# Fourteen of the mixer's sixteen transposed column blocks as seven block products, run beside the attention's steps, their results spilled to memory

## The chip, the cores and the metric

The kernel runs on one NeuronCore of a Trainium2 chip. The metric is the device time of one execution in microseconds (us). The kernel before takes 3112.58 us, the median of three runs (3110.77 to 3117.67).

The engines that matter here are PE (TensorE, the matrix products; PEld is its loading of weights), DVE (VectorE), ACT (ScalarE), POOL (GpSimd) and SP (SyncE, which issues most DMAs). Each works through its own instructions in a fixed order, and waits on semaphores for the others.

## The reference

Two layers, each a SwiGLU feed-forward network (FFN), a mixer and a second FFN, with RMS norms and per-sequence modulation around each. 640 tokens go through: 512 of a prompt and 8 x 16 of sampled sequences. D_MODEL is 1024. Of one mixer this matters:

```python
z = h @ w_in[l]                                   # (640, 1024) @ (1024, 5128)
q, k, v = z[AQ], z[AK], z[AV]                     # 512 columns each: attention, 4 heads
o_a = rmsnorm(attention(q, k, v, past_k, past_v)) # prompt: 512 tokens; sampled: 8 sequences on 256 past rows each
qk = silu(causal_conv(z[MQ : MV], conv0))         # 1024 columns: short convolution over tokens
vm, og = z[MV], sigmoid(z[MO])                    # 512 columns each
o_m = rmsnorm(og * mlstm(qk, vm, z[MI], z[MF], c0, n0, m0))   # 4 memory heads, new states returned
g = sigmoid(z[G])                                 # 2048 columns: a gate for each branch
y = (g[:1024] * (o_a @ w_pa[l]) + g[1024:] * (o_m @ w_pb[l])) @ w_out[l]
```

## The kernel before

**Numbers.** All products are in fp32 accuracy: both operands are split into a high part `hi` and a rest `lo`, and `three` (its matmuls appear at L91 or L80) adds hi*hi, hi*lo and lo*hi. The split of a weight tile is a copy on ACT and a subtraction on DVE (L300 for 128x1024, L330 and L495 for 128x512).

**Two ways to compute transposed columns.** Of `z`, the columns AQ, AK, MQ, MK and G are computed transposed (channels on partitions, tokens along the free dimension): 32 blocks of 128 columns, that is sixteen pairs of 256. `columns` computes a block plainly: for each of the two token halves of 320 it adds 8 x 3 matmuls of 128x320, so 48 per block and 96 per pair. The FFN has another way, `blocks` (L733): it cuts a pair's product into 2x2 blocks (tokens, columns, and the 1024 channels in halves of 512) and computes seven block products in place of eight, with sums on DVE and POOL before and after; a pair then takes 7 x 12 = 84 matmuls of 128x320. For this it needs sums of the input's blocks, which `split_half` and `combine` make (tiles `t42` and `t13`; the second fills the eight C tiles).

**One mixer's order.** In the program: AQ and AK of the first two heads, `values(0)` (token-major columns, and the gates MI and MF), the 8 prompt steps of the heads 0 and 1, AQ and AK of the heads 2 and 3, the other 8 prompt steps and the 8 sampled steps; `gate_columns(0)`; `values(1)`; MQ and MK columns, each followed by its convolution (`conv`); `values(2)`; `memory_gates`; the branch `w_pa`, with `gated`; the four memory heads (`memory_head`, `values(3)` within); `gate_columns(1)`; the branch `w_pb`, with `merge`; and `out_projection` with `w_out`. A scheduler orders each engine's instructions by this program and by priorities, so columns that stand later in the program fill PE between dependent steps that stand earlier. Tiles come from rings: `acc` and `bank` (PSUM), S (42 tiles), K (4 tiles of 128x320, `half`), W, X, C and raw; an instruction that takes a tile waits until the last reader of its predecessor in the ring is done.

**A memory head** is a chain of dependent parts: rows of the gates on PE, weights on DVE and ACT, five products `bank<-S,S` (queries by keys), the products with the values `bank<-S,Fv` and `bank<-X,Fp`, a norm on DVE, ACT and POOL, transposes (L1390), two copies to C tiles, and only then its part of `w_pb`. The new states (`bank<-S,Fa`, then L1430 on DVE, then a store) follow.

## Time and profile before

| | us |
|---|---|
| median of three runs | 3112.58 |
| the profiled execution | 3114.34 |
| its span | 3112.6 |
| mixer of layer 0, first column matmul to first `w_out` matmul (551.19 to 1055.34) | 504.1 |

The mean granted TensorE clock is 0.991. The mixer of layer 1 stands at about 2095 to 2600 us of the span and has the same shape. Within the mixer of layer 0, the sampled steps stand alone on PE from about 801 to 825 us, the convolutions run from about 831 us, the memory heads from 909.71 us, and `w_pb` from 1025 us. A stretch in which PE is busy for its whole length is bound by PE; where PE is idle, the releaser in brackets tells what it waited for. The busy time of a stretch counts overlapping rows once; the groups' busy times add them up.

### The profile page before, as it was taken

What the parts mean: (1) busy time and instruction counts of PE and PEld (TensorE: products, weight loads), DVE (VectorE), ACT (ScalarE), POOL (GpSimd) and SP (SyncE); (2) the same over time, 40 slices, a digit from 0 to 9 for tenths busy, and PEclk for the clock granted to TensorE, in tenths of its full rate; (3) what the DMA queues carried; (4) which work ended last, traced back from release to release, by engine and by line L of the source; (5) the groups of instructions that cost most, each with busy time, mean ns of one, the idle gap of its engine ahead of it and who ended that gap; (6) DMA issues with size and microseconds to landing.
All of it is one profiled execution on the core that took longest, in us unless ns stands there. A gap on an engine that the chain in (4) does not pass through costs nothing.

```text
span 3112.6 us, 51071 instructions
## 1 busy us (share of the span) xinstructions
PE 3014.8 (97%) x19101; PEld 2691.6 (86%) x19101; DVE 2002.8 (64%) x3745; ACT 1360.5 (44%) x2829; POOL 1040.5 (33%) x987
## 2 busy tenths in 40 slices
PE   6999999999999989999999999999999999899998
PEld 5888877999899979998778888879998998899986
DVE  5686557444675588785776665673446646887755
ACT  5333346344424364444643333562343334644454
POOL 3474304110111066660355552031001112676502
PEclk9999999999999999999999999999999999999999
DMA  7555536223323443334554555461233244333335
GB/s 231 159 177 167 186 125 219 88 79 92 116 77 115 131 161 109 122 106 139 177 183 155 172 164 170 140 215 55 82 99 106 77 124 156 104 89 89 105 126 176
DMA packets 307961, 417.47 MB, mean 134 GB/s; under 512 B 22235, under 2 KB 208967, under 8 KB 307714
## 3 DMA queue, kind: packets, MB, share of 16 engines
q1 hardware_dynamic: 303026, 402.78, 41.7%
q0 software_dynamic: 4688, 11.43, 1.1%
q8 instruction: 151, 2.47, 0.3%
q14 instruction: 96, 0.79, 0.1%
HBM read 386.98 MB, written 27.14 MB: 133 GB/s over the span
## 4 chain that ended last, share of the span: by engine, by line
PE 88%; DVE 5%; DMA 3%; ACT 2%; issue 1%; POOL 1%; SPq 0%; POOLq 0%; DVEq 0%; ACTq 0%
PE acc L91 53%; PE bank L91 29%; PE acc L80 4%; DMA raw<-in_w_ffn_dram 1%; DVE W L300 1%; ACT W L299 1%; DMA raw<-in_w_in_dram 1%; PE bank L1095 0%; DMA Fv<-in_w_ada_dram 0%; DVE S L495 0%; DMA S<-in_w_ada_dram 0%; PE bank L526 0%; DMA raw<-in_w_out_dram 0%; DVE S L556 0%; DVE X L593 0%
## 5 line engine op out<-in xcount | busy, mean ns | idle before, releaser
L91 PE MATMUL acc<-S,W 128*128 128x320 f32 x4640 | 747.4, 314 | 2.3 <-DVE dm L1182 1.6
L91 PEld LDWEIGHTS acc<-S,W 128*128 128x128 f32 x4640 | 688.7, 188 | 54.8 <-issue 22.7
L300 DVE TENSOR_TENSOR W<-raw,W 128x1024 fp32r<-128x1024 f32 x240 | 307.5, 1283 | 284.4 <-ACT W L299 282.9
L91 PE MATMUL acc<-W,C 128*128 128x512 f32 x1848 | 445.0, 400 | 15.0 <-DVE W L300 11.3
L91 PEld LDWEIGHTS acc<-W,C 128*128 128x128 f32 x1848 | 347.7, 190 | 109.6 <-DVE W L300 18.5
L299 ACT CAST W<-raw 128x1024 fp32r<-128x1024 f32 x248 | 259.7, 1048 | 358.8 <-PE acc L91 267.4
L495 DVE TENSOR_TENSOR W<-raw,W 128x512 fp32r<-128x512 f32 (+1 forms) x244 | 220.4, 904 | 153.2 <-ACT W L494 136.7
L91 PE MATMUL bank<-S,X 128*128 128x320 f32 x1936 | 315.4, 311 | 0.0
L91 PEld LDWEIGHTS bank<-S,X 128*128 128x128 f32 x1936 | 291.3, 188 | 10.9 <-issue 9.2
L91 PE MATMUL acc<-C,W 128*128 128x320 f32 x1728 | 274.1, 311 | 0.0
L91 PEld LDWEIGHTS acc<-C,W 128*128 128x128 f32 x1728 | 258.3, 188 | 5.1 <-issue 5.0
L801 POOL TENSOR_TENSOR S<-S,K 128x320 f32<-128x320 f32 x160 | 173.5, 1100 | 243.6 <-DVE K L800 238.4
L494 ACT CAST W<-raw 128x512 fp32r<-128x512 f32 (+1 forms) x244 | 150.7, 618 | 166.7 <-PE bank L91 77.6
L494 ACT CAST C<-S 128x384 fp32r<-128x384 f32 (+2 forms) x280 | 134.8, 490 | 126.4 <-PE acc L91 86.6
L495 POOL TENSOR_TENSOR C<-S,C 128x256 fp32r<-128x256 f32 x44 | 54.8, 1248 | 392.3 <-ACT C L494 391.8
L91 PE MATMUL bank<-W,C 128*128 128x512 f32 x792 | 185.1, 395 | 0.0
L91 PEld LDWEIGHTS bank<-W,C 128*128 128x128 f32 x792 | 149.0, 188 | 35.5
L495 DVE TENSOR_TENSOR X<-raw,X 128x512 fp32r<-128x512 f32 x160 | 161.5, 1011 | 25.6 <-ACT X L494 25.2
L451 POOL TENSOR_TENSOR sm<-sm,mhalf 128x1 f32<-128x1 f32 (+2 forms) x80 | 60.7, 759 | 345.3 <-DVE sm L446 175.6
L91 PE MATMUL acc<-S,X 128*128 128x320 f32 x976 | 166.4, 312 | 0.0
L91 PEld LDWEIGHTS acc<-S,X 128*128 128x128 f32 x976 | 148.2, 188 | 17.8 <-issue 10.9
L494 ACT CAST X<-raw 128x512 fp32r<-128x512 f32 (+1 forms) x164 | 100.6, 615 | 138.2 <-PE bank L91 92.5
(382 smaller groups left out, 5091.3 us busy)
## 6 DMA issues: line engine op xcount, KB each, us to landing
raw<-in_w_ffn_dram SPq DMA_DIRECT2D x348, 512.0 KB, 4.0
Fv<-in_w_ada_dram SPq DMA_DIRECT2D x261, 256.0 KB, 3.2
raw<-in_w_in_dram SPq DMA_DIRECT2D x72, 512.0 KB, 4.2
raw<-in_w_out_dram SPq DMA_DIRECT2D x32, 512.0 KB, 4.6
x<-X SPq DMA_DIRECT2D x25, 512.0 KB, 3.2
X<-x SPq DMA_DIRECT2D x25, 512.0 KB, 4.3
raw<-in_w_in_dram SPq DMA_DIRECT2D x32, 256.0 KB, 3.8
X<-in_cache_k_dram SPq DMA_DIRECT2D x16, 512.0 KB, 5.7
```

The costliest lines, as they stand in the source:

```text
L80: i = PE.matmul(out, lhsT, rhs, start=start and first is None, stop=stop and last is not None).ins
L91: i = PE.matmul(out, lhsT, rhs, start=start, stop=stop).ins
L299: ACT.copy(hi, src)
L300: (eng or DVE).tensor_tensor(lo, src, hi.bitcast(F32), ALU.subtract)
L451: pows.append(POOL.tensor_tensor(r, t, mhalf.to_broadcast([P, n]), ALU.pow).ins)
L494: ACT.copy(hi, src)
L495: (eng or DVE).tensor_tensor(lo, src, hi.bitcast(F32), ALU.subtract)
L801: POOL.tensor_tensor(gm, gm, z, ALU.mult)
```

## The change

**Which columns.** Only the first pair of AQ and the first of AK stay plain (`first_columns`, with weights that are split early). The other fourteen pairs (AQ and AK of the heads 2 and 3, all of G, MQ and MK) go through `blocks(..., apart=True)`: its weights take W tiles alone, its sums an X tile, its products `acc` tiles alone. `pre_norm` therefore always leaves the plain sum in `x`, and `split_half` and `combine` run for the mixer too, as for the FFN.

**Where they run.** `side_blocks` is a generator with two turns per pair. One turn is taken after each turn of the attention's steps (`turns` is the old `pipeline`, turn by turn): four before `values(0)` of the attention's second half, and the rest beside the remaining prompt steps and all sampled steps.

**Where the results go.** AQ and AK stay in S tiles. The gates' tanh (16 blocks) and the convolution's input (8 blocks) are written to memory in halves of 128x320 (160 KB) by SP (`to_memory`, through a K tile), and loaded back as 320 KB tiles by `gated`, `merge` and `conv`. Since the C tiles hold the block sums until the last pair is done, the attention's normed rows are put aside in memory by POOL's queue (`put_aside`, six per layer), and `attention_out` loads, transposes and splits them after the stage. The tables of masks are loaded in two lots. S tiles become 645 wide.

**What follows later.** History, `values(0)`, both `conv`, `values(1)`, `attention_out`, `memory_gates`, `conv_rows`, `values(2)`, `w_pa`, the memory heads (with `values(3)`) and `w_pb` stand after the stage, without MQ, MK and gate columns among them.

Counted over the program, PE has 336 fewer matmuls of 128x320, DVE 3873 rows in place of 3666, ACT 2537 in place of 2446, POOL 1083 in place of 951, and SP 1157 in place of 993 (among them 96 stores of 160 KB and 48 loads of 320 KB).

```diff
+    def combined(h):
+        for k in range(HK):
+            h["t42", k] = O(), O()
+            h["t4", k], h["t2", k] = ([z[:, c] for z in h["t42", k]] for c in halves_of_tokens)
+            h["t13", k] = C(), C()
+            h["t1", k], h["t3", k] = ([z[:, c] for z in h["t13", k]] for c in halves_of_tokens)
+        return h
...
-    def blocks(src, h, put):
+    def blocks(src, h, put, apart=False):
...
-            x = WX((P, 2 * HK, P), F32R)
+            x = (W if apart else WX)((P, 2 * HK, P), F32R)
             hl = x[:, :HK], x[:, HK:]
             split_to(hl, t, eng)
-            out = product_bank()
+            out = acc()[:, :TA] if apart else product_bank()
...
+        if apart:
+            s12 = X((P, 2 * HK, P))
+            s1, s2 = s12[:, :HK], s12[:, HK:]
+        else:
+            s1, s2 = (F("a").rearrange("p (k c) -> p k c", k=HK) for _ in range(2))
...
+        def first_columns(puts):
+            ws = list(zip(puts, first_weights["mixer", l]))
+            for t in range(2):
+                for put, w in ws:
+                    b = acc()[:, :TA]
+                    proj_t(b, w, h, t)
+                    put(t, b)
...
+        def to_memory(dst, m0, finish=None):
+            def put(m, t, x, y, over):
+                z = x if over else half()
+                DVE.tensor_tensor(z, x, y, ALU.add)
+                if finish:
+                    finish(z)
+                load(dst[m0 + m][:, halves_of_tokens[t]], z)
+            return put
+        gate = [spilled(f"tanh_{br}", KD) for br in range(2)]
+        pre = spilled("pre", KD)
+        def side_blocks():
+            def keep(dst, scale=None):
+                def put(m, t, x, y, over):
+                    if 2 + m not in dst:
+                        dst[2 + m] = L()
+                    o = dst[2 + m][:, halves_of_tokens[t]]
+                    DVE.tensor_tensor(o, x, y, ALU.add)
+                    if scale:
+                        ACT.activation(o, o, AF.Copy, scale=scale[2 + m])
+                return put
+            def half_tanh(z):
+                ACT.activation(z, z, AF.Tanh, scale=0.5)
+            parts = [(OFF_AQ + 256, keep(q, qscale)), (OFF_AK + 256, keep(k))]
+            parts += [(OFF_G + DM * br + P * m, to_memory(gate[br], m, half_tanh)) for br in range(2) for m in range(0, KD, 2)]
+            parts += [(OFF_MQ + P * m, to_memory(pre, m)) for m in range(0, KD, 2)]
+            for off, put in parts:
+                yield from blocks(wl[:, off:off + 256], h, put, apart=True)
...
+        def put_aside(j):
+            aux(aside[j], rms_rows(obs[j]))
...
-            xn = rms_rows(obs[hd])
-            yield
-            tr = rows_t(xn)
-            oa[hd] = C(), C()
-            ACT.activation(oa[hd][0][:, :SEQ], tr, AF.Copy, scale=na)
-            DVE.scalar_tensor_tensor(oa[hd][1][:, :SEQ], tr, na, oa[hd][0][:, :SEQ].bitcast(F32), ALU.mult, ALU.subtract)
+            put_aside(hd)
...
+        def attention_out():
+            for hd in range(NH):
+                xn = F("a")
+                load(xn, aside[hd])
+                tr = rows_t(xn)
...
+            for m in range(4):
                 mm_ = base + m
-                if not half:
-                    zt[m] = L(), mk(per, [P, 152], "dm", 1)
-                z, zs = zt[m]
-                zs = zs.rearrange("p (b t) -> p b t", b=SB)
-                if not half:
-                    POOL.memset(z[:, 0:3], 0.0)
-                    POOL.tensor_copy(zs[:, :, 0:3], hT[:, mm_].rearrange("p (b j) -> p b j", b=SB))
-                    ACT.copy(z[:, 3:3 + TA], b)
-                    return
-                ACT.copy(z[:, 3 + TA:515], b[:, :SEQ - TA])
-                DVE.tensor_copy(zs[:, :, 3:], b16(b[:, SEQ - TA:]))
+                z, zs = L((P, 3 + TOK)), once([P, 152], "dm").rearrange("p (b t) -> p b t", b=SB)
+                POOL.memset(z[:, 0:3], 0.0)
+                load(z[:, 3:], pre[mm_])
+                POOL.tensor_copy(zs[:, :, 0:3], hT[:, mm_].rearrange("p (b j) -> p b j", b=SB))
+                DVE.tensor_copy(zs[:, :, 3:], b16(z[:, 3 + SEQ:]))
...
-        attn_columns(0)
-        values(0)
-        history()
+        attn_columns()
+        attn_values(0)
         for hd in (0, 1):
             head_rows(hd)
-        pipeline([prompt_step(hd, i) for hd in (0, 1) for i in range(4)])
-        attn_columns(1)
+        steps = turns([prompt_step(hd, i) for hd in range(NH) for i in range(4)] + [sampled_step(b) for b in range(SB)])
+        side = side_blocks()
+        for n in range(4):
+            next(side)
+            next(steps)
+        attn_values(1)
         for hd in (2, 3):
             head_rows(hd)
         key_rows(NH)
-        pipeline([prompt_step(hd, i) for hd in (2, 3) for i in range(4)] + [sampled_step(b) for b in range(SB)])
-        ta = gate_columns(0)
+        for _ in itertools.zip_longest(side, steps):
+            pass
+        history()
+        _, _, tri = table(1)
+        tri_b, mask_w, mask_wb, mask_t, mask_tb = table(2)
+        values(0)
+        conv(0, qm, 0.5)
         values(1)
-        columns(*halves_at(OFF_MQ, 512, conv(0, qm, 0.5)))
-        columns(*halves_at(OFF_MK, 512, conv(4, km, 0.5 * KSCALE)))
-        values(2)
+        conv(4, km, 0.5 * KSCALE)
+        attention_out()
         mem = memory_gates()
         conv_rows()
+        values(2)
         def gated(m, a, b):
+            ta[m] = L()
+            load(ta[m], gate[0][m])
...
-        tb = gate_columns(1)
-        h2 = new_rows()
+        h2 = plain_rows()
         def merge(m, a, b):
+            tb = L()
+            load(tb, gate[1][m])
```

**PE beside a prompt step** (layer 0). Before: between a step's transposes and scores (`bank`) stand plain columns of AQ for the heads 2 and 3, `acc_6673`, from the input's tiles `S`, and their weights `W`.

```order
L91 MATMUL acc_6673<-S_4140,W_6668 128x320
L91 MATMUL acc_6673<-S_4142,W_6667 128x320
L1053 MATMUL bank_6327<-ident_63,Fp_6310 128x128 x2
L91 MATMUL bank_6334<-S_5817,S_5763 128x384
L91 MATMUL bank_6338<-S_5817,S_5763 128x384
L91 MATMUL acc_6673<-S_4143,W_6667 128x320
L91 MATMUL acc_6673<-S_4142,W_6668 128x320
L91 MATMUL acc_6673<-S_4144,W_6667 128x320
```

After, the same kind of step (`bank_6949` is its transpose, `bank_6956` and `bank_6960` its scores):

```order
L91 MATMUL acc_7016<-S_4158,W_7013 128x320
L91 MATMUL acc_7016<-S_4160,W_7013 128x320
L91 MATMUL acc_7016<-S_4161,W_7013 128x320
L1073 MATMUL bank_6949<-ident_63,Fp_6869 128x128 x2
L91 MATMUL bank_6956<-S_5835,S_5781 128x384
L91 MATMUL bank_6960<-S_5835,S_5781 128x384
L91 MATMUL acc_7016<-S_4160,W_7013 128x320
L91 MATMUL acc_7035<-S_4162,W_7032 128x320
L91 MATMUL acc_7035<-S_4163,W_7032 128x320
```

The filling matmuls are now those of block products: a product is twelve matmuls, so `acc_7016` ends here, and `acc_7035` begins the next one with another split weight tile.

**VectorE at the end of `values(0)` of the memory.** Before: the splits of the next column block's weights (`W_6546`, `W_6605`) stand around the copies of the five token tiles (`acc_6090` to `bank_6094`), and nothing of the convolution is near.

```order
L330 TENSOR_TENSOR W_6546<-raw_6541,W_6545 128x512
L330 TENSOR_TENSOR W_6546<-raw_6543,W_6545 128x512
L986 COPY S_6231<-acc_6090 128x128
L986 COPY S_6231<-acc_6091 128x128
L986 COPY S_6231<-acc_6092 128x128
L989 TENSOR_TENSOR gt_5728<-acc_6090,bif_5729 128x8
L986 COPY S_6231<-acc_6093 128x128
L989 TENSOR_TENSOR gt_5728<-acc_6091,bif_5729 128x8
L986 COPY S_6231<-bank_6094 128x128
L989 TENSOR_TENSOR gt_5728<-acc_6092,bif_5729 128x8
L1158 COPY S_5736<-bank_6251 128x192
L330 TENSOR_TENSOR W_6605<-raw_6541,W_6604 128x512
```

After, `S_9416` is a convolution input loaded from memory, and `S_9424` its sum:

```order
L299 TENSOR_TENSOR W_9499<-raw_9495,W_9498 128x1024
L1001 COPY S_9396<-acc_9255 128x128
L1001 COPY S_9396<-acc_9256 128x128
L1001 COPY S_9396<-acc_9257 128x128
L1004 TENSOR_TENSOR gt_5714<-acc_9255,bif_5715 128x8
L1001 COPY S_9396<-acc_9258 128x128
L1004 TENSOR_TENSOR gt_5714<-acc_9256,bif_5715 128x8
L1001 COPY S_9396<-bank_9259 128x128
L1004 TENSOR_TENSOR gt_5714<-acc_9257,bif_5715 128x8
L299 TENSOR_TENSOR W_9566<-raw_9562,W_9565 128x1024
L1203 COPY dm_9417<-S_9416 128x8x16
L1210 TENSOR_SCALAR S_9424<-S_9416,cwb_5728 128x512
```

The convolution's first instructions (L1203, L1210) stand behind the copies L1001 of `values(0)`, while their input comes from memory.

**PE in the memory heads.** Before, in the last two heads: `bank` tiles are the heads' own products and transposes, `acc_10529` a gate column block.

```order
L91 MATMUL bank_10101<-S_8681,S_8995 128x128
L91 MATMUL acc_10529<-S_4144,W_10523 128x320
L91 MATMUL acc_10529<-S_4145,W_10523 128x320
L91 MATMUL acc_10529<-S_4144,W_10524 128x320
L91 MATMUL bank_10106<-S_8681,S_8995 128x128
L91 MATMUL acc_10529<-S_4146,W_10523 128x320
L91 MATMUL bank_10111<-S_6232,Fa_10109 128x128 x4
L91 MATMUL bank_10111<-ws_9279,S_6232 128x1 x4
L91 MATMUL bank_10111<-wsm_9283,S_6232 128x8
L1400 MATMUL bank_10129<-ident_63,S_8839 128x128 x4
L1400 MATMUL bank_10135<-ident_63,S_8839 128x128
L1390 MATMUL bank_10140<-ident_63,S_9144 128x128 x4
```

After, head 2: `bank_10765` to `bank_10787` are its five products `S,S`, `bank_10812` its products with the values, and `acc_11260` a part of `w_pb` for head 0.

```order
L91 MATMUL acc_11260<-C_10527,W_11219 128x320
L91 MATMUL acc_11260<-C_10526,W_11220 128x320
L91 MATMUL bank_10765<-S_9462,S_9690 128x512
L91 MATMUL bank_10771<-S_9462,S_9690 128x384
L91 MATMUL bank_10777<-S_9462,S_9690 128x256
L91 MATMUL bank_10782<-S_9462,S_9690 128x128
L91 MATMUL bank_10787<-S_9462,S_9690 128x128
L1420 MATMUL bank_10790<-ident_63,S_9652 128x128 x4
L1420 MATMUL bank_10796<-ident_63,S_9652 128x128
L1410 MATMUL bank_10801<-ident_63,S_9630 128x128 x4
L1410 MATMUL bank_10808<-ident_63,S_9630 128x128
L91 MATMUL bank_10812<-S_10092,Fv_10759 128x129 x2
```

The column blocks between a head's parts are gone; what is left between them is other heads' own work and the first heads' part of `w_pb`.

## Rows read from the trace of the kernel before

**Rows 1.** The page of the profile: busy time by engine, and the chain that ended last
```profile
PE 3014.8 (97%) x19101; PEld 2691.6 (86%) x19101; DVE 2002.8 (64%) x3745; ACT 1360.5 (44%) x2829; POOL 1040.5 (33%) x987
...
PE 88%; DVE 5%; DMA 3%; ACT 2%; issue 1%; POOL 1%; SPq 0%; POOLq 0%; DVEq 0%; ACTq 0%
```

**Rows 2.** Busy time by stretch: start:end, length, PE, PEld, DVE, ACT, POOL, clock, DMA
```profile
551.00:1055.00 504.00, 495.59 (x3795) 471.28 (x3795) 274.46 (x777) 187.11 (x491) 61.45 (x116) 1.00 0.31 95
801.00:831.00 30.00, 25.34 (x300) 21.20 (x300) 13.35 (x54) 13.07 (x36) 2.46 (x6) 1.00 0.41 123
831.00:1055.00 224.00, 224.00 (x1696) 218.74 (x1695) 149.44 (x408) 79.70 (x201) 35.21 (x68) 1.00 0.34 102
940.00:1025.00 85.00, 85.00 (x642) 82.72 (x641) 40.80 (x107) 31.76 (x90) 10.38 (x13) 1.00 0.41 123
1033.00:1055.00 22.00, 22.00 (x152) 21.99 (x151) 20.13 (x44) 8.32 (x15) 1.82 (x3) 1.00 0.39 122
1120.00:1130.00 10.00, 8.49 (x38) 7.46 (x39) 7.76 (x19) 10.00 (x27) 4.75 (x7) 0.66 0.55 188
1140.00:1150.00 10.00, 5.44 (x29) 4.92 (x29) 10.00 (x11) 6.18 (x13) 9.57 (x10) 0.90 0.02 7
1200.00:1250.00 50.00, 50.00 (x342) 48.91 (x340) 41.01 (x57) 22.03 (x40) 34.16 (x24) 1.00 0.35 105
```

**Rows 3.** Timeline of PE in the sampled steps: start, length, work, [idle before, releaser]
```profile
816.76 0.91 PE L91 MATMUL bank<-dm,Fa 128*128 128x128 f32 x6 [0.72 <-ACT C L1144]
...
822.05 0.91 PE L91 MATMUL bank<-dm,Fa 128*128 128x128 f32 x6 [1.03 <-DVE dm L1117]
```

**Rows 4.** Groups by form on VectorE from 831 to 1055 us: busy, mean ns, idle before
```profile
L300 DVE TENSOR_TENSOR W<-raw,W 128x1024 fp32r<-128x1024 f32 x13 | 15.9, 1223 | 7.0 <-ACT W L299 7.0
L330 DVE TENSOR_TENSOR W<-raw,W 128x512 fp32r<-128x512 f32 x20 | 13.2, 688 | 7.3 <-ACT W L329 7.3
...
L1462 DVE SCALAR_TENSOR_TENSOR S<-S,acc 128x320 f32<-128x320 f32 x16 | 7.7, 483 | 5.5 <-PE acc L91 5.4
...
L1422 DVE TENSOR_TENSOR Fa<-S,wsm 128x512 f32<-128x512 f32 x8 | 5.5, 687 | 3.3 <-DMA out_dram<-Fa 3.3
```

**Rows 5.** Groups by form on PE from 831 to 1055 us
```profile
L91 PE MATMUL acc<-S,W 128*128 128x320 f32 x574 | 92.5, 316 | 0.0
L91 PE MATMUL acc<-C,W 128*128 128x320 f32 x382 | 58.2, 311 | 0.0
L80 PE MATMUL acc<-W,S 128*128 128x256 f32 x192 | 28.5, 291 | 0.0
```

**Rows 6.** Timeline of VectorE in the convolution: where one row begins before another's end
```profile
837.96 0.69 DVE L1007 TENSOR_TENSOR Fa<-bank,sm 128x512 f32<-128x512 f32 x1
838.56 0.28 DVE L1182 COPY dm<-acc 128x128 f32<-128x128 f32 x1
```

**Rows 7.** Timeline of PE over the memory heads
```profile
909.71 1.03 PE L1318 MATMUL bank<-ident,X 128*128 128x128 f32 x8
...
925.84 1.02 PE L91 MATMUL bank<-S,S 128*128 128x512 f32 x2
...
934.55 2.62 PE L91 MATMUL bank<-S,Fv 128*128 128x129 f32 x22
...
939.08 2.00 PE L91 MATMUL acc<-S,W 128*128 128x320 f32 x12
...
971.38 2.62 PE L91 MATMUL bank<-S,Fv 128*128 128x129 f32 x22
973.93 0.65 PE L91 MATMUL bank<-X,Fp 128*32 128x129 f32 x16
...
983.60 0.60 PE L1390 MATMUL bank<-ident,S 128*128 128x128 f32 x4
```

**Rows 8.** DMA issues from 551 to 1055 us: KB each, median us to landing
```profile
out_dram<-S POOLq DMA_DIRECT2D x5, 256.0 KB, 2.8
...
x<-X SPq DMA_DIRECT2D x2, 512.0 KB, 2.6
```

**Rows 9.** Timeline of PE at the mixer's start, and at the FFN's start behind it
```profile
568.49 0.66 PE L526 MATMUL bank<-ident,Fa 128*128 128x128 f32 x4 [2.04 <-DVE Fa L521]
...
1147.90 2.50 PE L91 MATMUL acc<-S,C 128*128 128x320 f32 x8 [3.17 <-DVE S L495]
```

More of the change, by code (lines that the diff above doesn't have):

```diff
@@ L356, in begin @@
         for j, c in enumerate(cols):
-            out.append(early_chunks(c, slots if j < 2 else O))
+            if key[0] == "mixer" and j == 3:
+                t = raw()[:, :KD * P].rearrange("p (k c) -> p k c", k=KD)
+                load(t, c.rearrange("(k p) c -> p k c", p=P))
+                out.append(list(zip(*([x[:, k] for k in range(KD)] for x in split(t, (KD, P))))))
+            else:
+                out.append(early_chunks(c, slots if j < 2 else O))
             yield
@@ L511, in combine @@
             split_to(h["t42", k], x2)
-        for k in range(HK):
-            split_to(h["t13", k], x[k])
+            split_to(h["t13", k], x1)
     def htok(h, i):
@@ L614, in rows_out @@
         last = ph == 3 * depth - 1
-        forms = not last and nxt[0] != "mixer"
-        x = new_x() if forms else None
-        h = None if last else (new_forms if forms else new_rows)()
+        x = None if last else new_x()
+        h = None if last else (new_rows if nxt[0] == "mixer" else new_forms)()
         early = iter(()) if last else begin(nxt, slots)
@@ L650, in rows_out @@
                 if 1 in fs:
-                    post_norm(ph, i, *ygs[i], y[i, 1], gi, x, h, mod)
-            if forms and fs == (1,):
+                    post_norm(ph, i, *ygs[i], y[i, 1], gi, x, mod)
+            if not last and fs == (1,):
                 split_half(h, x, 0)
-            if not last and fs == (1,):
                 next(early)
-        if forms:
+        if not last:
             split_half(h, x, 1)
@@ L819, in ffn, with turns @@
         return down(ph, w_ffn2[l, f], gt, g, mods.get(nxt), (l + 1, 0) if f else ("mixer", l))
[L822 removed]
+    def turns(steps):
         under_way = []
@@ L828, in pipeline @@
             under_way = [x for x in under_way + [s] * (s is not None) if next(x, x) is not x]
+            yield
+    def pipeline(steps):
+        for _ in turns(steps):
+            pass
     def mixer(l, ph, h, nxt):
@@ L858, in mixer @@
         nm = nam[:, depth + l:depth + l + 1]
-        def columns(*parts, early=False):
-            part_b = []
-            def finish():
-                for put, m, w in part_b:
-                    b = acc()
-                    proj_t(b[:, :TB], w, h, 1)
-                    put(m, 1, b[:, :TB])
-                part_b.clear()
-            ready = iter(first_weights["mixer", l] if early else ())
-            for off, put, m0 in parts:
-                if not early:
-                    r = halves_of_k(wl[:, off:off + 256])
-                for e in range(2):
-                    w = next(ready) if early else chunks(r, e)
-                    a = acc()
-                    proj_t(a[:, :TA], w, h, 0)
-                    put(m0 + e, 0, a[:, :TA])
-                    part_b.append((put, m0 + e, w))
-                    if not early:
-                        finish()
-            finish()
@@ L886, in halves_at @@
-        def halves_at(off, n, put):
-            return [(off + P * m, put, m) for m in range(0, n // P, 2)]
-        token_half = slice(0, TA), slice(TA, TOK)
-        def gate_columns(br):
-            out = {}
-            def put(m, half, y):
-                if not half:
-                    out[m] = L()
-                ACT.activation(out[m][:, token_half[half]], y, AF.Tanh, scale=0.5)
-            columns(*halves_at(OFF_G + DM * br, DM, put))
-            return out
+        def first_columns(puts):
[5 more added lines that the diff above has]
+                    put(t, b)
@@ new lines, in mixer, with spilled @@
+        token_half = halves_of_tokens
+        def spilled(name, n):
+            return [dram.tile([P, TOK], F32, name=f"{name}_{l}_{m}") for m in range(n)]
+        def to_memory(dst, m0, finish=None):
[7 more added lines that the diff above has]
+        gate = [spilled(f"tanh_{br}", KD) for br in range(2)]
@@ L1008, in rms_rows @@
             return xn
+        aside = [dram.tile([P, 512], F32, name=f"aside_{l}_{j}") for j in range(NH + 2)]
+        def put_aside(j):
+            aux(aside[j], rms_rows(obs[j]))
         def rows_t(xn):
```

139 lines of the change are left out of this document (65 added, 74 removed).

## The prediction

> **What bounds the kernel now.** I read the page first: PE is busy for 97% of the span and makes 88% of the chain that ended last [rows 1]. So time goes only by taking work from PE, or by filling the few places where it is idle. Then the busy time by stretch, for the mixer of layer 0 [rows 2]: PE is busy for 495.6 of 504.0 us. Of the 8.4 us of idle time 4.7 lie between 801 and 831 us (25.34 of 30.00), where the sampled steps stand alone; the timeline there shows a wait of 0.72 us for ACT and one of 1.03 us for VectorE before a step's product with `dm` [rows 3]. From 831 to 1055 us PE is busy without a gap, while VectorE is busy for 149.4 of 224 us and ACT for 79.7: no other engine is the bound there, but `w_pb` from 1033 us on has VectorE at 20.13 of 22 us. Everything below is per layer; the second mixer has the same shape, so it counts twice.
>
> **What the change takes away.** Fourteen pairs lose 12 matmuls of 128x320 each, 168 in all. In a stretch with nearly only such matmuls 342 took 50.00 us, 0.1462 us each [rows 2]. In a stretch bound by PE that is 168 x 0.1462 = 24.6 us. The sampled steps now have side products between their dependent parts, so their 4.7 us of idle time go. Together 29.3 us; both I hold for sure as long as the stage beside the attention stays bound by PE.
>
> **The stage beside the attention.** A pair is 84 matmuls, 84 x 0.1462 = 12.3 us of PE. VectorE has for it seven splits of 128x512 at 0.688 us and some six sums of 128x320 at 0.483 us (priced like L1462) [rows 4], 7.7 us. The sampled steps alone take 13.35 us of VectorE on 25.34 us of PE [rows 2], so their sum stays near 60% of PE's. What can hold it is a ring: four K tiles serve the sums, and a spilled half gives its tile back only when its store has landed. A store like these took 2.6 to 2.8 us [rows 8], against some 3 us of PE for a quarter of a pair. That fits, but the stores stand in SP's one order behind loads of weights and of cached keys, which wait for their own tiles. I take 3 us, between 0 and 10.
>
> **The start.** The sums of the input's blocks are new here. Four plain blocks (192 matmuls, 28 us) and the attention's value columns stand before the first product that needs them. The mixer's start already waits 2.04 us for VectorE; the FFN behind it, which has less ahead of the same sums, waits 3.17 us for a split [rows 9]. I take 1.5 us, between 0 and 4.
>
> **The stretch after the stage** is where I look for the loss. In the kernel before, the columns of MQ, MK and the second gate lie among the dependent parts of the convolution and of the memory heads. From 831 to 1055 us PE has 574 + 382 = 956 matmuls of 128x320 [rows 5]; the two branches are 384 of them, so 572 are such columns, 572 x 0.1462 = 84 us. They now stand earlier, and two more `values` come into the stretch. A `values` is 120 matmuls of 128x256, at 28.5 us for 192 [rows 5] at most 17.8 us; I take 16. PE's work in the new stretch is then about 224 - 84 + 32 = 172 us.
>
> VectorE's work: 149.4 us, less the splits of twelve column blocks (12 x 1.2 = 14 us [rows 4]), plus two `values` (9 us, two splits of 1.223 and ten small copies each) and about 10 us of the convolution and of the attention's last copies that stood before 831 us (an estimate by the same rows): 155 us. To this comes a wait: behind the copies of `values(0)` in VectorE's order stand the convolution's instructions, so VectorE has nothing to do for some 12 us of that product's 16. That is 167 us against 172. VectorE is not the bound over the whole stretch, but it has no slack either, and what counts is where a dependent chain has nothing beside it:
> - At the hand-over: `values(1)` needs tiles that VectorE's copies of `values(0)` free, about 1 us; in `w_pa` the second product needs the tile of `values(2)`, freed behind a queue of convolution and gate instructions, about 3 us. I take 4 us, 1 to 7.
> - Heads 0 and 1 still have `values(3)` beside them, and took from 909.71 to 939.08 us with PE full [rows 7]. But the last convolution instructions now stand between their parts on VectorE. I take 2 us, 0 to 4.
> - Heads 2 and 3 lose their cover. From a head's first product `S,S` to its first `S,Fv` the shortest case shown is 925.84 to 934.55, 8.7 us; PE has some 4 us of its own to do meanwhile (five products, ten transposes), so 4 to 5 us are bare, twice. From the end of `X,Fp` to the transposes of the norm of the last head go 974.6 to 983.6 us, 9.0 us [rows 7], against some 5.5 us of PE work of the other head, state products and `w_pb`; 3.5 us more. That would be 12 to 13 us; as VectorE has fewer splits in its queue than before, I take 10, 6 to 16.
> - The end of `w_pb`: the new states, formerly spread from 974 us on, now come within it. VectorE was at 20.13 of 22 us without most of them, and L1422 had waited 3.3 us for stores of its `Fa` tiles [rows 4]. State products give PE work too. I take 4 us, 0 to 9.
>
> **The clock.** [...] A stretch of 10 us at 0.66 gives away 3.4 us. Some gaps in the heads will be longer than those of the sampled steps; part of what they cost falls on time that waits anyway. I take 1.5 us, 0 to 4.
>
> **The sum** per layer: 1.5 + 3 + 4 + 2 + 10 + 4 + 1.5 = 26 us of new idle time against 29.3 us gained: 3.3 us less, 6.6 us for both layers. The profiled execution took 3114.3 us (span 3112.6), which is 1.8 us above the median; taken from the median 3112.6 the forecast is 3106 us. All lower ends together make 7 us, so 45 us less (3068); all upper ends 54 us, so 49 us more (3162).
>
> **Rivals.**
> - *The cover was not needed.* Other heads' parts, states and `w_pb` fill the gaps, as PE can begin any head whose inputs are there. For it: VectorE and ACT at 149 and 80 of 224 us are far from full [rows 2]. Against it: each engine keeps its written order, and the order of the heads 2 and 3 leaves little between. Then some 11 us are lost per layer, and 2 x 18.3 = 37 are gained: 3076 us.
> - *VectorE becomes the bound of the stretch.* I count its instructions as overlapping: one that lasts 0.69 us was followed by the next after 0.60 us [rows 6]. If that gain goes where each waits for another engine, its some 390 instructions need 0.085 us more each, 33 us: 155 + 33 + 12 = 200 us against PE's 172. Then 28 us are idle there, and with 4.5 us of the earlier terms and 2.5 of tile waits the layer loses 35 against 29.3: slower, 3112.6 + 2 x 5.7 = 3124 us. It decides from about 16 us of lost overlap. For it: `w_pb` at 20.13 of 22. Against it: at that load PE had no gap. [...]
> - *The clock falls at each bare gap of the heads.* Four gaps, each with a stretch like that at 0.66 behind it, cost 4 x 3.4 = 14 us in place of my 1.5: 38.5 us lost per layer against 29.3, slower, 3112.6 + 2 x 9 = 3131 us. For it: the drop behind the stall before the FFN. Against it: 1.00 through the gaps of the sampled steps [rows 2, 3]. [...]
> - *The stores hold the stage.* If each of the twelve spilled pairs waits once for a store, 2.7 us [rows 8], the stage loses 32 us per layer in place of 3: 3106 + 58 = 3164 us. Against it: four K tiles, and nothing in the trace shows SP's order late there.
>
> **Chances.** The forecast's own case 0.46 (its own range 3094 to 3120), the cover not needed 0.20, VectorE the bound 0.22, the clock 0.05, the stores 0.07. A measurement of this kernel can tell about 0.2% (6 us) from no change. The forecast lies right at that bound: of its 0.46 I give 0.25 to faster, 0.13 to no change, 0.08 to slower. The second case is all faster, the third 0.19 slower and 0.03 no change, the last two slower: faster 0.45, no change 0.16, slower 0.39. The range 3074 to 3134 us takes in the first four cases but for their ends.
>
> **What would show it.** PE without gaps in the sampled steps and 1176 matmuls of 128x320 per layer in side products confirm the gain; `acc` products waiting for K sums or W splits there refute my 3 us. PE's idle time between the end of the stage and `w_out` should be about 20 us per layer, half of it in heads 2 and 3 before `S,Fv` and before the transposes of the norm. If it is under 8 us, the first rival holds; if VectorE is busy without gaps from `values(1)` to `w_out`, the second. A wait of PE over 5 us that ends on a store to memory would make the prediction wrong in a way that I hold unlikely.

## The result, and the profile after

The changed kernel is slower: 3138.48 us (median of 4, 3134.3 to 3140.47) against 3112.56 us (3110.77 to 3117.67) in the same comparison, a ratio of 1.0079 with a 95% interval of 1.0061 to 1.0096. The profiled execution has a span of 3132.6 us, 20.0 more than the 3112.6 of before; it is the quickest of the four, so the profile accounts for 20.0 of the 25.9 us between the medians.

The page's first row of the changed kernel, busy time by engine, has 336 PE instructions fewer than [rows 1] (168 per mixer), but PE's busy time fell by only 25.6 us and its share from 97 to 95%:

```profile
PE 2989.2 (95%) x18765; PEld 2648.2 (85%) x18765; DVE 2200.2 (70%) x3959; ACT 1423.6 (45%) x2923; POOL 1211.8 (39%) x1119
```

The windows of the changed kernel (columns as in [rows 2]): first its mixer of layer 0, from the first product to the first of `w_out`, then the start, the stage beside the attention with what follows it up to `w_pa`, and the late stretch from 929 us on; then four stretches of 10 us at waits.

```profile
553.07:1066.85 513.78, 482.80 (x3629) 450.95 (x3629) 377.27 (x910) 219.22 (x538) 146.88 (x185) 0.98 0.42 129
553.00:600.00 47.00, 38.78 (x257) 37.65 (x258) 32.11 (x56) 18.45 (x42) 20.76 (x25) 0.89 0.17 55
600.00:929.00 329.00, 317.94 (x2437) 295.87 (x2435) 237.41 (x527) 149.82 (x362) 101.43 (x109) 0.99 0.45 139
929.00:1067.00 138.00, 126.25 (x937) 117.60 (x938) 107.91 (x329) 51.02 (x136) 24.69 (x51) 0.98 0.43 130
570.00:580.00 10.00, 3.44 (x16) 2.58 (x15) 8.41 (x14) 4.71 (x12) 6.18 (x9) 0.61 0.01 2
780.00:790.00 10.00, 6.30 (x45) 4.91 (x46) 7.02 (x14) 4.16 (x9) 3.21 (x3) 0.66 0.36 90
930.00:940.00 10.00, 7.10 (x39) 6.84 (x38) 9.63 (x43) 1.91 (x4) 0.41 (x2) 0.83 0.27 83
1050.00:1060.00 10.00, 9.13 (x59) 9.06 (x58) 6.41 (x17) 2.19 (x4) 0.55 (x1) 0.83 0.36 113
```

The mixer takes 513.8 us where [rows 2] has 504.0: 9.8 us more, twice that in two layers. Of it PE is idle for 31.0 us, where it was 8.4. Its busy time fell by 12.8 us, not by the 24.6 us that 168 matmuls cost at full clock, so PE is busy for 11.8 us more than its matmuls account for. The sum closes: 22.6 - 12.8 = 9.8.

Part of the 11.8 us is a lower clock. These are all stretches of that mixer at a granted clock of 0.50, and last the only one of the kernel before:

```profile
572.11:582.35 10.24, 4.68 (x18) 4.15 (x17) 10.07 (x16) 4.61 (x11) 6.96 (x8) 0.50 0.01 2
780.32:787.15 6.83, 3.45 (x24) 2.46 (x25) 3.86 (x5) 2.22 (x6) 2.89 (x3) 0.50 0.34 99
933.93:937.34 3.41, 3.17 (x12) 3.17 (x13) 3.35 (x17) 1.12 (x3) 0.21 (x1) 0.50 0.00 0
1053.39:1056.80 3.41, 3.41 (x15) 3.41 (x14) 2.20 (x7) 0.88 (x2) 0.00 (x0) 0.50 0.87 266
...
571.06:574.48 3.42, 3.36 (x12) 3.11 (x13) 2.31 (x12) 1.42 (x8) 2.34 (x2) 0.50 0.02 5
```

PE is busy in them for 14.7 us, before for 3.4. Half of that is the most that the clock can have taken, 7.4 against 1.7 us, so 5.7 of the 11.8 us (an estimate from these rows). The other 6.1 us are at full clock. PE's timeline lists 21 waits of 0.2 us or more in this mixer, where it listed 7, and a matmul that stands alone has a longer row (0.42 us at 614.35) than each adds in a full stretch (0.146): 14 more such ends would make some 4 us (an estimate from these two figures). How the rest comes about no run shows.

PE's timeline in that mixer, the entries with a wait of some length (in brackets: idle time before, and what ended it):

```profile
569.78 0.66 PE L535 MATMUL bank<-ident,Fa 128*128 128x128 f32 x4 [1.60 <-DVE Fa L530]
573.71 0.90 PE L91 MATMUL acc<-S,S 128*128 128x320 f32 x2 [1.47 <-ACT S L504]
578.70 12.18 PE L91 MATMUL acc<-S,S 128*128 128x320 f32 x70 [4.09 <-DVE S L505]
...
778.51 1.07 PE L1110 MATMUL bank<-ident,X 128*128 128x128 f32 x8 [2.59 <-DMA X<-in_cache_k_dram]
783.70 1.62 PE L91 MATMUL bank<-dm,Fa 128*128 128x128 f32 x6 [4.12 <-DVE dm L1132]
...
934.17 8.43 PE L91 MATMUL acc<-C,W 128*128 128x320 f32 x46 [2.90 <-ACT S L1002]
998.73 0.49 PE L91 MATMUL bank<-S,S 128*128 128x128 f32 x2 [1.07 <-DVE Fv L1369]
...
1024.90 0.77 PE L1410 MATMUL bank<-ident,S 128*128 128x128 f32 x5 [1.20 <-DVE S L1402]
1065.32 1.16 PE L91 MATMUL bank<-S,Fa 128*128 128x128 f32 x8 [1.82 <-DVE Fa L1442]
```

There are three places. **The start** (578.70): PE waits 4.09 us for VectorE's split of the mixer's input, behind shorter waits of 1.60, 1.00 and 1.47 us. **The first sampled steps** (778.51, 783.70): 2.59 us for a key load and 4.12 us for the weights `dm` of a sampled step, just where the side products were to give cover; the other sampled steps are closed, as forecast. **The stretch after the stage**, from 929 us on: one wait of 2.90 us for the second product of `w_pa`, and many short ones behind it, 11.75 us in all. Layer 1 repeats them (waits of 4.10, 2.69, 4.04 and 2.90 us).

How the second place comes about is to be read on POOL's timeline of the changed kernel (start, length, line, work):

```profile
734.18 1.30 POOL L757 TENSOR_TENSOR X<-raw,raw 128x512 f32<-128x512 f32 x1 [9.52 <-DVE sm L1061]
...
771.27 0.09 POOL L861 MEMSET cp<- 128x1 f32 x1 [19.96 <-DVE sm L1067]
776.59 1.04 POOL L455 TENSOR_TENSOR sm<-sm,mhalf 128x4 f32<-128x4 f32 x1 [5.22 <-DVE sm L450]
777.61 1.26 POOL L757 TENSOR_TENSOR X<-raw,raw 128x512 f32<-128x512 f32 x1
778.88 0.60 POOL L117 DMA_DIRECT2D aside<-Fa  x1
779.50 1.28 POOL L758 TENSOR_TENSOR X<-X,raw 128x512 f32<-128x512 f32 x1
```

POOL forms the weight sums of a side pair (L757, L758) in a tile `X`. The ring of that name has three tiles, and a sampled step takes two of them, for its keys and for their transposes. Behind the pair whose sums begin at 734.18 us no other pair's begin for 43 us, and for 20 us before 771 POOL does nothing. POOL's own last wait here is put down to VectorE (5.22 us, before L455), as the sums stand behind that instruction in POOL's order; that the ring is what holds them is an inference from the code, which e3 and e11 test. Until the sums come, at 777.61, no product of the next pair can be made: PE's timeline has no `acc` product between 771.96 and 787.75 us. So each of the two kinds of work that were to cover each other stands without cover there.

### The profile page after: what moved, and what is told of

Read it like the earlier page. It is cut to its first block, busy times and chain, and to the rows that moved or that the text cites. A ratio compares the mean times of both kernels' runs of the same rounds, so it can differ in the third digit from the quotient of the medians.

```text
span 3132.6 us, 51454 instructions
## 1 busy us (share of the span) xinstructions
PE 2989.2 (95%) x18765; PEld 2648.2 (85%) x18765; DVE 2200.2 (70%) x3959; ACT 1423.6 (45%) x2923; POOL 1211.8 (39%) x1119
## 5 line engine op out<-in xcount | busy, mean ns | idle before, releaser
L91 PE MATMUL acc<-S,W 128*128 128x320 f32 x3728 | 601.2, 312 | 6.6 <-DVE K L747 2.3
L91 PEld LDWEIGHTS acc<-S,W 128*128 128x128 f32 x3728 | 554.2, 188 | 55.4 <-ACT W L504 23.1
L505 DVE TENSOR_TENSOR W<-raw,W 128x512 fp32r<-128x512 f32 (+1 forms) x384 | 327.7, 854 | 168.3 <-ACT W L504 153.1
L298 ACT CAST W<-raw 128x1024 fp32r<-128x1024 f32 x250 | 262.5, 1050 | 323.6 <-PE acc L91 200.7
L91 PE MATMUL acc<-C,W 128*128 128x320 f32 x2400 | 394.3, 315 | 10.2 <-ACT S L1002 6.4
L91 PEld LDWEIGHTS acc<-C,W 128*128 128x128 f32 x2400 | 363.4, 191 | 23.3 <-issue 9.8
L504 ACT CAST W<-raw 128x512 fp32r<-128x512 f32 (+1 forms) x384 | 236.6, 619 | 244.3 <-PE acc L91 141.8
L91 PEld LDWEIGHTS bank<-S,X 128*128 128x128 f32 x1936 | 291.6, 188 | 10.9 <-issue 8.4
L455 POOL TENSOR_TENSOR sm<-sm,mhalf 128x1 f32<-128x1 f32 (+2 forms) x80 | 63.9, 799 | 302.8 <-DVE sm L450 149.5
L764 POOL TENSOR_TENSOR raw<-raw 128x512 f32<-128x512 f32 x108 | 177.1, 1640 | 0.5
L757 POOL TENSOR_TENSOR Fa<-raw,raw 128x512 f32<-128x512 f32 x80 | 112.8, 1410 | 140.7 <-DMA raw<-in_w_ffn_dram 101.3
```

Source lines behind the costliest of these rows:

```text
L91: i = PE.matmul(out, lhsT, rhs, start=start, stop=stop).ins
L298: ACT.copy(hi, src)
L455: pows.append(POOL.tensor_tensor(r, t, mhalf.to_broadcast([P, n]), ALU.pow).ins)
L504: ACT.copy(hi, src)
L505: (eng or DVE).tensor_tensor(lo, src, hi.bitcast(F32), ALU.subtract)
L757: POOL.tensor_tensor(s1, a21, a22, ALU.add)
```

## The experiments

Each was run in the same comparison as the kernel before, whose median was 3112.6 to 3115.7 us. The letters in the quoted expectations name theories. Most are told where they stand, and A is another one from run to run: in e2 that the way of the splits over ScalarE and VectorE holds the start, in e3, e4, e8 and e11 that the ring `X` is short. F says that the sums of `combine` stand ahead of the last splits at the start, G that the stretch behind the stage lacks independent matmuls. "Idle" and "clock" below are of layer 0's mixer, from its first product to the first of `w_out`.

| kernel | median us | ratio to before (95%) | idle us | PE busy us, matmuls | clock |
|---|---|---|---|---|---|
| the change | 3138.48 | 1.0079 (1.0061 to 1.0096) | 31.0 | 482.8, 3629 | 0.98 |
| e1 plain columns beside | 3141.75 | 1.0091 (1.0070 to 1.0113) | 16.2 | 501.1, 3796 | 0.99 |
| e2 direct start | 3139.98 | 1.0080 (1.0053 to 1.0107) | 31.2 | 482.5, 3629 | 0.98 |
| e3 sums in `raw` | 3105.19 | 0.9969 (0.9958 to 0.9980) | 20.5 | 477.0, 3629 | 0.99 |
| e4 stores on POOL's queue | 3136.97 | 1.0074 (1.0054 to 1.0094) | 32.0 | 484.6, 3629 | 0.97 |
| e5 = e3 + sums behind splits | 3097.22 | 0.9938 (0.9927 to 0.9950) | 17.7 | 475.7, 3629 | 0.99 |
| e6 = e3 + second gate late | 3090.31 | 0.9923 (0.9911 to 0.9934) | 13.5 | 478.0, 3676 | 0.99 |
| e7 = e5 + second gate late | 3084.60 | 0.9903 (0.9890 to 0.9916) | 10.8 | 476.4, 3676 | 1.00 |
| e8 = e5 + keys a turn earlier | 3098.40 | 0.9951 (0.9938 to 0.9964) | 18.0 | 479.2, 3628 | 0.98 |
| e9 = e7 with two pairs late | 3065.85 | 0.9842 (0.9828 to 0.9855) | 7.3 | 470.9, 3628 | 1.00 |
| e10 = e7 with three pairs late | 3072.41 | 0.9871 (0.9857 to 0.9884) | 9.6 | 476.4, 3664 | 0.99 |
| e11 = e7 with sums in `X` | 3110.04 | 0.9987 (0.9978 to 0.9996) | 19.7 | 481.6, 3676 | 0.98 |

In e9 some 25 small products of the mixer stand behind the first of `w_out`, so its row leaves them out; it has 24 column matmuls more than the change, as two pairs are plain.

**e1: the same place, but plain columns.** Is the saving by block products real, and are they to blame?

```diff
...
-                yield from blocks(wl[:, off:off + 256], h, put, apart=True)
+                r = halves_of_k(wl[:, off:off + 256])
+                for e in range(2):
+                    w = chunks(r, e)
+                    for t in range(2):
+                        b = acc()[:, :TA]
+                        proj_t(b, w, h, t)
+                        put(e, t, None, b, False)
+                    yield
```

> The fourteen pairs stay beside the attention's steps and are spilled as in the changed kernel, but each is computed plainly: 96 matmuls of 128x320 in place of 84; the block sums are still made at the start, and not used. Theory A (the saving is real, and stalls with a halved clock behind them eat it): 168 more matmuls per layer at 0.1462 us are 24.6 us, 49 us in all; a plain block needs no sums in an X tile, so the stall at the first sampled steps (6.7 us idle and some 3 us of halved clock per layer) should go: 3138 + 49 - 20 = about 3167 us. Theory B (the products save little there, since PE waits or runs slower beside the attention): within 10 us of the changed kernel or faster, 3110 to 3148 us.

Without sums in `X` the stage beside the attention has no wait of 1 us or more; the start's wait (3.71 us) and the late stretch remain. The kernel is as slow as the change, as 168 matmuls per layer are back. So the move alone costs time: with as many matmuls as before, 26 us against the 3115.65 us of the kernel before in that comparison. And the stall comes with the block products; which part of them brings it, e3 tells.

**e2: the start without its detour.** `pre_norm` writes the two parts of the input directly, so that no split follows.

```diff
+            if h:
+                for q in range(4):
...
+                    hh, hl = (z[:, at] for z in h[k])
...
+                    (POOL if q == 3 else DVE).tensor_tensor(hl, x[k][:, at], hh.bitcast(F32), ALU.subtract)
```

> Only the mixer's start is changed back: the norm before it writes the input's high and low parts tile by tile, as in the kernel before, beside the plain sum that the block sums need; split_half is left out there. Theory A: the start's idle time falls from 8.2 to about 3.6 us per layer and the 10.2 us of halved clock behind it to 3.4, so 4.6 + 3 = about 8 us per layer, 3138 - 16 = 3122 us. Theory C (the start is late for another reason, the extra copies on ACT and VectorE, or what is gained is lost at the next wait): 3135 to 3142 us.

Nothing was gained; the start's waits are 1.89, 2.64 and 3.66 us. As I had put it, A falls: the same amount of work is only written elsewhere, and the last part still comes late on VectorE.

**e3: the weight sums in a tile of the `raw` ring**, which the sampled steps don't use.

```diff
-            s12 = X((P, 2 * HK, P))
+            s12 = raw()[:, :KD * P].rearrange("p (k c) -> p k c", k=KD)
```

> Only one tile is changed: the side products' weight sums lie in a raw tile in place of an X tile, whose ring of three also holds the sampled steps' cached keys and their transposes. Theory A: the first sampled step's keys are loaded earlier, and the next pair's sums don't wait for an X tile; the idle 2.6 + 4.1 us near 778 and 784 us and the 6.8 us of halved clock behind them go, some 9 us per layer, 3138 - 18 = 3120 us. Theory D (the load of the keys is late because SP's order holds it behind the stores): the wait stays, 3135 to 3142 us. A raw ring that is now too short would show as a wait for raw or W tiles and make it slower.

33 us less than the change, where 18 were expected. POOL's timeline of this kernel, in the same place as above:

```profile
741.79 1.30 POOL L757 TENSOR_TENSOR raw<-raw,raw 128x512 f32<-128x512 f32 x1 [6.68 <-DVE sm L1057]
...
757.11 1.60 POOL L757 TENSOR_TENSOR raw<-raw,raw 128x512 f32<-128x512 f32 x1 [5.98 <-DMA raw<-in_w_in_dram]
...
772.18 1.69 POOL L757 TENSOR_TENSOR raw<-raw,raw 128x512 f32<-128x512 f32 x1 [1.14 <-DVE W L505]
773.94 1.62 POOL L758 TENSOR_TENSOR raw<-raw,raw 128x512 f32<-128x512 f32 x1
```

A pair's sums come at 742, 757 and 772 us, without the pause of 43 us. PE's timeline there, and the window of 10 us that had 0.66:

```profile
777.11 1.78 PE L91 MATMUL acc<-S,W 128*128 128x320 f32 x11
...
782.86 1.06 PE L1110 MATMUL bank<-ident,X 128*128 128x128 f32 x8 [1.20 <-DMA X<-in_cache_k_dram]
783.68 6.55 PE L91 MATMUL acc<-S,W 128*128 128x320 f32 x43
```

```profile
780.00:790.00 10.00, 8.80 (x73) 8.30 (x66) 6.70 (x18) 5.79 (x18) 2.87 (x3) 1.00 0.74 237
```

The key load is still waited for (1.20 us), but 6.55 us of side products stand behind it, the wait for `dm` is gone and the clock stays at 1.00. In the mixer as a whole PE has 10.5 us less idle time and 5.8 us less busy time than in the change. Of the idle time 6.1 us went beside the attention (5.0 are left from 600 to 918 us) and 2.5 us at the start: the change's waits of 1.60 and 1.00 us there are 0.16 us in this kernel, and e11, with the sums back in `X`, has 1.45 and 0.99. The norm in front of the mixer takes tiles of that ring too, and the first pair's sums run on POOL as early as 554.68 us.

Against e1, which has a wait like the change's at the start (3.71 us) and a late stretch like it, PE is busy for 24.2 us less, at the same granted clock of 0.99: that is the saving by 168 matmuls, forecast as 24.6.

**e4: the spilled halves stored by POOL's queue** in place of SP's.

```diff
-                load(dst[m0 + m][:, halves_of_tokens[t]], z)
+                aux(dst[m0 + m][:, halves_of_tokens[t]], z)
```

> Only the queue of the spill stores is changed: POOL issues them in place of SP. Theory D (the stores hold up SP's order, and with it the loads of keys and weights): the stall near 778 to 784 us goes and the loads come earlier, 3138 - 18 = about 3120 us. Theory A (the X ring is what holds the loads): within 5 us of the changed kernel, 3133 to 3143 us, or slower where POOL's sums now wait behind stores.

No change beyond the interval; the waits at the first sampled steps stay (3.00 and 3.72 us). So the stores' place in SP's order is not the cause. The K tiles, the forecast's other limit, were not changed in any run; in the change no wait of PE, VectorE or ScalarE from 553 to 929 us is put down to one of these stores.

**e5: e3, and the sums of `combine` behind the last splits.** In the changed kernel VectorE and POOL start these sums (L517, L518), which only the third block product needs, among the splits that the first plain products wait for. VectorE's timeline of that kernel at the start:

```profile
573.52 0.68 DVE L517 TENSOR_TENSOR S<-S 128x320 f32<-128x320 f32 x1
...
575.24 0.88 DVE L517 TENSOR_TENSOR S<-S 128x320 f32<-128x320 f32 x2
...
577.51 4.79 DVE L505 TENSOR_TENSOR S<-S,S 128x320 fp32r<-128x320 f32 x5
```

```diff
...
+            if "mixer" in h:
+                in_order(i, h["last", False], "behind the splits")
+                in_order(j, h["last", True], "behind the splits")
```

> Sums in a raw tile as in e3 (3105 us), and at the mixer's start VectorE and POOL are told to begin the block sums (combine) only behind the last splits of the input rows (split_half). Theory F (the start waits since combine's sums stand between those splits, and its sums on POOL stretch the splits on VectorE: 4.79 us for five rows of 128x320): the wait of 4.03 us before the second token half falls to about 1 us and the halved clock behind it from 6.8 to 3.4 us, some 5 us per layer, 3095 us. Theory C (the start is late for the norm's own chain, or the first side products then wait for their sums): 3102 to 3108 us.

8 us less than e3. VectorE's and PE's timelines of e5: the splits are one block from 572.77 us, the sums follow, and PE's wait of 4.09 us (4.03 in e3) has become 1.11 us. F holds. It has two parts, the order and the stretching of VectorE's splits beside POOL's sums (five in 4.79 us above, six in 3.83 here); the run doesn't part them.

```profile
572.77 3.83 DVE L505 TENSOR_TENSOR S<-S,S 128x320 fp32r<-128x320 f32 x6
576.53 1.97 DVE L518 TENSOR_TENSOR S<-S 128x320 f32<-128x320 f32 x3
...
574.37 12.08 PE L91 MATMUL acc<-S,S 128*128 128x320 f32 x70 [1.11 <-DVE S L505]
```

**e6: e3, and the second gate's four pairs again plain columns**, behind the memory heads.

```diff
+        for m in range(0, KD, 2):
+            r = halves_of_k(wl[:, OFF_G + DM + P * m:OFF_G + DM + P * m + 256])
+            for e in range(2):
+                w = chunks(r, e)
+                tb[m + e] = L()
+                for t in range(2):
+                    b = acc()[:, :TA]
+                    proj_t(b, w, h, t)
...
-            load(tb, gate[1][m])
```

> Sums in a raw tile as in e3, and the four pairs of the second gate go back behind the memory heads in the program, as plain columns kept in S tiles: ten pairs are left beside the attention. Theory G (the late stretch is slow for want of cover): its 12.6 us of idle time per layer and the halved clock of 6.8 us there mostly go, 10 + 3 us, against 4 x 12 x 0.1462 = 7 us of matmuls given back: 6 us less per layer, 3105 - 12 = 3093 us. Theory H (the waits are chains that columns cannot fill in the written order): plus 7 us per layer, 3119 us.

15 us less than e3, though 48 matmuls per layer (7.0 us) came back. Windows of the sampled steps and of the late stretch of e6:

```profile
800.00:830.00 30.00, 25.02 (x305) 20.66 (x301) 12.65 (x56) 11.11 (x32) 2.07 (x7) 0.98 0.65 198
918.00:1046.00 128.00, 128.00 (x971) 124.26 (x971) 77.45 (x204) 51.43 (x143) 16.04 (x24) 1.00 0.39 118
```

PE has no gap in the late stretch, at a clock of 1.00; e3's stretch of 136 us from 918 us on had 125.94 busy at 0.97. G holds. In exchange the sampled steps, with only ten pairs beside, run out of cover: 25.02 of 30 us busy, as in [rows 2].

**e7: e5 and e6 together**, so the diff is that of both:

```diff
+                in_order(i, h["last", False], "behind the splits")
...
+        for m in range(0, KD, 2):
+            r = halves_of_k(wl[:, OFF_G + DM + P * m:OFF_G + DM + P * m + 256])
```

> e5 and e6 together. If both theories F and G hold and are independent: 3105 - 10 - 12 = 3083 us. If only F: 3109; if only G: 3093; if neither, 3119 us.

The gains add: 3084.6 us, where 8.0 and 14.9 us less than e3 would make 3082.3.

**e8: e5, with each sampled step's keys loaded one turn earlier** (the edit against e5).

```diff
             load(kc, cache_k[l, b].rearrange("(j p) h e -> p j (h e)", p=P))
+            yield
```

> e5, and each sampled step issues the load of its cached keys one turn earlier. In e3 one wait of 1.2 us for the first keys was left per layer: at most 2.4 us less than e5. If the X ring of three is the tight resource (theory A), a key tile held one turn longer makes the steps wait for X tiles and it gets slower than e5, by some us.

No gain over e5. PE's wait for the first keys fell from 1.51 to 0.91 us, too little for the time to show.

**e9 and e10: e7 with only two or three late plain pairs**, so that twelve or eleven pairs stand beside the attention and reach into the sampled steps. The edit of e9 against the change, without that of e7:

```diff
...
-            parts += [(OFF_G + DM * br + P * m, to_memory(gate[br], m, half_tanh)) for br in range(2) for m in range(0, KD, 2)]
+            parts += [(OFF_G + DM * br + P * m, to_memory(gate[br], m, half_tanh)) for br in range(2) for m in range(0, KD if br == 0 else KD - 2 * 2, 2)]
```

> e7 (3084.6 us) with only the last two pairs of the second gate plain behind the memory heads, twelve beside the attention. In e7 the sampled steps stand alone again at the end (5.0 us idle per layer) and the late stretch has no idle time. If the two pairs fill both: 2 x 12 x 0.1462 = 3.5 us fewer matmuls and up to 5 us less idle time, 3084.6 - 2 x 8.5 = 3068 us; if two pairs (28 us of PE) are too little cover for the heads, some 6 us per layer come back there: 3080 us.

> The same with three pairs plain, eleven beside the attention. 1.75 us fewer matmuls per layer than e7 and up to 5 us less idle time in the sampled steps: 3084.6 - 2 x 6.5 = 3072 us where three pairs cover the heads, 3080 us where they don't.

e9 beats both kernels: 3065.85 us, a ratio of 0.9842 to before (0.9828 to 0.9855), 48 us. Its windows from 600 us to shortly behind the mixer's last product:

```profile
600.00:900.00 300.00, 295.62 (x2312) 277.06 (x2311) 224.44 (x542) 139.37 (x340) 86.83 (x103) 1.00 0.48 148
900.00:1040.00 140.00, 139.86 (x1060) 133.61 (x1059) 103.04 (x300) 58.48 (x152) 26.22 (x48) 1.00 0.39 120
```

Both the stage and the stretch behind it are now nearly full, at full clock: 4.4 and 0.1 us idle. Two plain pairs, 192 matmuls, are cover enough for the heads; a third (e10) costs 6.6 us more.

**e11: e7 with the sums back in `X`.** What is the ring worth when all else is mended? The edit against e7:

```diff
-            s12 = raw()[:, :KD * P].rearrange("p (k c) -> p k c", k=KD)
+            s12 = X((P, 2 * HK, P))
```

> e7 with the weight sums back in the X ring: late block sums and four plain pairs, but the tile of the changed kernel. Theory A (the X ring costs what e3 gained, 33 us, wherever it stands): 3084.6 + 33 = 3117 us. If the ring costs time only where the stage is crowded by fourteen pairs: 3085 to 3100 us.

25 us more than e7. PE's timeline in e11 has the pair of waits of the change again:

```profile
779.33 1.94 PE L1116 MATMUL bank<-ident,X 128*128 128x128 f32 x8 [3.24 <-DMA X<-in_cache_k_dram]
783.92 1.62 PE L91 MATMUL bank<-dm,Fa 128*128 128x128 f32 x6 [2.65 <-DVE dm L1138]
```

## Why the prediction was wrong

**The gain was right.** 24.6 us per layer were forecast for the matmuls, and e3 against e1 shows 24.2. The sampled steps' idle time of 4.7 us went too, except in the first two.

**The idle time was nearly right in sum**, by luck. The losses without the clock were 24.5 us by the forecast, less 4.7 that go: 8.4 + 24.5 - 4.7 = 28.2 us of idle time per mixer, and 31.0 were measured. But they lie elsewhere:

| term, per layer | forecast us | measured us |
|---|---|---|
| start | 1.5 (0 to 4) | 4.6 (8.2 idle, 3.6 before) |
| stage beside the attention | 3 (0 to 10) | about 10.9 |
| hand-over | 4 (1 to 7) | 3.3 |
| heads 0 and 1 | 2 (0 to 4) | 0 |
| heads 2 and 3 | 10 (6 to 16) | 4.4 |
| end of `w_pb` | 4 (0 to 9) | 4.2 |
| clock | 1.5 (0 to 4) | 11.8 of busy time, at most 5.7 by the clock |

**The step that failed is the stage beside the attention**, priced at 3 us with 10 as its upper end. I looked at the four K tiles and at the stores in SP's order; e4 clears that order. The ring that counts is `X`, with three tiles, for which the weight sums of the new pairs and the sampled steps compete; the diff shows it in one line (`s12 = X(...)`), and the forecast did not list who else takes from that ring. e3 prices it at 33 us over both layers, 10.5 us of idle and 5.8 us of busy time per layer, and e11 at 25 us where ten pairs stand beside. The 33 us are the whole of what the forecast missed (3138 - 3106 = 32). With that one line changed, e3 takes 3105 us, the forecast almost to the microsecond; but that is luck in part, as its late stretch has 10.1 us of idle time where 20 were forecast, and its busy time is 6.0 us above 495.6 - 24.6 where 1.5 were.

**The other term that failed is the clock**, the only term for busy time of PE beyond its matmuls: 1.5 us with 4 as its upper end, and 11.8 measured. The lower clock accounts for at most 5.7 us of it; the other 6.1 us, at full clock, had no term in the forecast, which let a wait cost its own length alone. The 1.5 us were my estimate beside the 3.4 us that the 0.66 of [rows 2] (1120 to 1130 us) gives away; no run shows them by themselves. I had tied the term to "some gaps in the heads", taking [rows 2, 3] to say that gaps of about 1 us leave the clock alone. For most gaps that holds: the sampled steps of e6 and e7, which stand alone again, kept 0.98 and 0.94, and the change's stretches from 600 to 770 us and from 983 to 1050 us, with seven waits of 0.97 to 1.22 us, have 1.00. It doesn't hold for all: the stretch from 1053.39 us on has 0.50 behind a wait of 0.87 us, and why it fell there and not in the heads is open. The forecast had no new waits of 2.6 to 4.1 us in the start and in the stage, and three of the four stretches at 0.50 hold such a wait or follow one.

The rival built on the clock gave 3131 us, the nearest to the result, with a chance of 0.05. That was luck: it gave the clock 14 us per layer where at most 7.4 show, and looked at the gaps of the heads, where the whole stretch of 138 us has 0.98. e5 against the change shows waits and busy time falling together: with the same 3629 matmuls it has 13.3 us less idle time and 7.1 us less busy time, of which the lower clock can be at most 2.5 (14.7 us busy at 0.50 in the change, 9.6 in e5).

**The start's wait was sized too small by its order.** I counted the sums as work that four plain blocks cover, which they do; I did not look at where they stand on VectorE, ahead of splits that PE waits for at once. e5 shows it: moved behind them, 3 us of wait per layer go, and 8 us of time in all.

**The loss behind the stage was half of what I feared**, 11.75 us of idle time for hand-over, heads and `w_pb` where 20 were forecast. It is one of cover: the columns were cheap work in the right place, and e6 shows that giving back 7 us of it per layer returns more than it costs. VectorE was not the bound there: 107.91 us busy of 138, and in e9 the same stretch is full with 103.04 of 140 us on VectorE. That rival falls, and that of the stores in SP's order too.

**Open.** The cost of the shared ring is not split further: the wait for the key load, the sums that came late, the start's short waits and the small VectorE instruction below were all changed by the same one-line edit.

## What to carry to other kernels

When work is moved beside other work to cover it, list every ring of tiles that both take from, with its length and its order: if they share one, they may not cover each other. Here a wait cost more than its length: 22.6 us more idle time came with 11.8 us more busy time, at most half of it by the clock, which was 0.50 for 3.4 us or more in or behind each wait of 2.6 to 4.1 us, once behind a wait of 0.87 us, and 1.00 over the stretches with seven waits of 0.97 to 1.22 us. And cheap independent matmuls are a resource: leave as many of them as the dependent stretch needs (here two pairs of fourteen) before turning the rest into something faster.

## What the runs showed that was not expected

A VectorE instruction on 128x1 elements that takes 0.15 to 0.16 us in all 16 steps of the kernel before took 2.54 us in the changed kernel at 780.69 us, while two sums of 128x512 ran on POOL (and 2.45 us in the same place of layer 1). VectorE's and POOL's timelines of the changed kernel there:

```profile
780.69 2.54 DVE L1130 TENSOR_TENSOR sm<-sm,cs 128x1 f32<-128x1 f32 x1
783.27 0.29 DVE L1132 TENSOR_SCALAR dm<-S,sm 128x128 f32<-128x128 f32 x1
791.35 0.16 DVE L1130 TENSOR_TENSOR sm<-sm,cs 128x1 f32<-128x1 f32 x1
...
780.72 1.27 POOL L764 TENSOR_TENSOR raw<-raw 128x512 f32<-128x512 f32 x1
781.95 1.26 POOL L771 TENSOR_TENSOR raw<-raw,X 128x512 f32<-128x512 f32 x1
```

It begins 0.03 us before the first sum of POOL and ends at 783.23, within 0.03 us of the end of the second; the instruction behind it is the one that ended PE's wait of 4.12 us. The 2.4 us by which it is longer lie within that wait; what made it so long no run here tried by itself.
